# A one-column float32 matmul in front of nine of a transformer block's weight products

## The chip, the cores and the metric

The kernel runs on one core of a Trainium2 chip. The metric is the device time of one execution in microseconds. Where it is given for several runs, the median stands first and the lowest and highest behind it.

## The reference

One encoder block on 256 tokens of 2048 features, everything in float32. Cut to what matters:

```python
h = rms_norm(x, attn_norm)
proj = h @ w_in                       # 2048 x 10240: queries, keys, values, two gates
qa, ka, va, qb, kb, vb, ga, gb = jnp.split(proj, split_points, axis=-1)
ya = windowed_gqa(qa, ka, va, rel_bias_table, sink_a)        # 8 heads on 2 keys/values
yb = dilated_attention(qb, kb, vb, rel_bias_table)           # 3 groups of 4 heads
merged = sigmoid(ga) * (ya @ w_branch_a) + sigmoid(gb) * (yb @ w_branch_b)
x = x + merged @ w_out
hf = rms_norm(x, ffn_norm)
g = dwconv_centred(hf @ w_ffn_gate, conv_w, conv_b)          # 2048 x 5632
x = x + (gelu(g) * (hf @ w_ffn_up)) @ w_ffn_down
gate_p = sigmoid(rms_norm(x, ple_norm) @ w_ple_gate)
x = x + gate_p * (p @ w_ple_proj)
return rms_norm(x, final_norm)
```

## The kernel before

All weights are streamed once, in blocks of 128 by 128. A piece of 16 blocks arrives by DMA in two tiles named raw (lines 231 to 247). Each block is split into a high part whi (a ScalarE copy into the reduced float32 type, line 261) and the rest wlo (a VectorE subtraction, line 262), and the activations are kept in the same two parts. A product of two float32 matrices is then made of three products of parts: high by high, high by low, low by high.

The work is a list of jobs, _JOBS, made by _plan() and walked in order by the loop at line 1003. A job is one product with its weights. Two kinds of job matter here:

- The ordinary product (lines 330 to 335) has one block column of weights: a query or key head, or 128 features of the MLP's gate ("g") or up ("u") projection. It takes a PSUM accumulator acc of 512 columns out of three and calls block() 16 times, once for each 128 of the 2048 inputs. block() (lines 318 to 328) issues two matmuls with the weights as the stationary operand: line 324, whi against 512 columns (both parts of the 256 tokens), and line 325, wlo against the 256 columns of the high part.
- The wide product (lines 349 to 385) has the activations as the stationary operand and up to 512 columns of weights as the moving one: the values ("v"), the attention gates, the branches and the last stage. Lines 359 to 361 are its three matmuls. The products with w_out and w_ffn_down are made in a similar way by seven_product (lines 387 to 441; lines 410 to 412).

The order of the jobs is: seven queries and keys together (the first stage), values, the remaining queries of the first attention, keys, queries and values of the second attention in turn, the gates and branches, w_out ("o"), the MLP's first half (three gate products together, "gg", and then gate and up products in turn), w_ffn_down's first half ("d0"), the MLP's second half, which starts at job _HALF, w_ffn_down's second half ("d1"), and the per-layer embedding. A job's aftermath (soft-max, transposes at line 685 and at line 878, norms) is put into later jobs: at((i, k), f) asks that f be called before block k of job i, and run_due calls it. So short groups of other matmuls stand in the middle of a product: the sums of squares at line 472 (float32, one column each), the spreading of a norm at line 500 (float32, 256 columns), the scores and values of the attention at lines 631 to 644 and 700.

Each engine has one queue. The order within a queue is made by a planner that walks the instructions by priority and by planned times. keep (line 223) pins an instruction behind the one issued before it on the same engine. Semaphores are placed by the framework. ones is a 128 by 128 float32 tile of ones in SBUF (line 205).

Of the kernel before, what the change touches and what calls it, by code (L numbers as in the profile page):

```python
# [125 lines left out]
def _pairs(kind, c):  # L126

    if kind == "o":
        return ([2, 4, 5, 6, 7, 0, 1, 3] if c else [0, 1, 2, 4, 5, 6, 7, 3]), range(LATER, LATER + 4)
    if kind == "d1" and c == 1:  # L130
        return [5, 0, 1, 6, 2, 3, 7, 4, 8, 9, 10], range(5)
    return [8, 0, 1, 2, 3, 9, 4, 5, 6, 7, 10], range(SAVED)


FIRST = 7
START = FIRST + 1
_JOBS = _plan()
WARM = 9
_HALF = next(i for i, j in enumerate(_JOBS) if j[0] == "g" and j[1] == FHALF)


def _stream():
# [47 lines left out]
def _encoder(ctx: ExitStack, tc, xt, pt, cols, table, onehot, mask, ident_in, last_gain, wts, xrows, out):  # L190
    nc = tc.nc
# [13 lines left out]
    ones = const.tile([P, P], F32, name="ones")  # L205
# [17 lines left out]
    keep = tc.keep_in_program_order  # L223
# [94 lines left out]
    def block(acc, m, first, last, ahead=3):  # L318

        b = state["at"]  # L320
        s, o = _SUB_OF[b]
        split_to(s + ahead)
        hi, lo = subs[s]
        nc.tensor.matmul(acc, hi[:, o, :], m, start=first, stop=False, skip_group_check=True)  # L324
        nc.tensor.matmul(acc[:, T:], lo[:, o, :], m[:, :T], start=False, stop=last, skip_group_check=True)  # L325
        state["at"] = b + 1
        if o == _SUBS[s][1] - 1:
            del subs[s]

    def product(i, moving, n):  # L330
        acc = ps.tile([P, 2 * T], F32, name="acc", bufs=3)
        for k in range(n):
            run_due(i, k)
            block(acc, moving(k), k == 0, k == n - 1)
        return acc

    def products_by_halves(i, moving):

        accs = []
        for b in range(TOGETHER * KC):  # L340
            (h, e), k = divmod(b // SUB, TOGETHER), b % SUB
            run_due(i, b)
            if h + k == 0:
                tag = "sp" if e < 2 else "acc"
                accs.append(ps.tile([P, 2 * T], F32, name="acc", tag=tag, bufs=2 if e < 2 else 3))
            block(accs[e], moving(SUB * h + k), h + k == 0, h == 1 and k == SUB - 1)
        return accs

    def wide_product(i, still, n, w, tag, places=HALVES, late=0):

        accs = [ps.tile([P, W4], F32, name="acc", tag=tag, bufs=3 if tag == "acc" else 2) for _ in places]

        def step(k, t, hi, lo):
            xh, xl = (still(k)[:, c:c + T][:, places[t]] for c in (0, T))
            acc = accs[t][:, :w * P]
            nc.tensor.matmul(acc, xh, hi, start=(k == 0), stop=False)  # L359
            nc.tensor.matmul(acc, xh, lo, start=False, stop=False)  # L360
            nc.tensor.matmul(acc, xl, hi, start=False, stop=(k == n - 1 - t * late))  # L361

        later = []
        for k in range(n):
            run_due(i, k)
            b = state["at"]
            s, o = _SUB_OF[b]
            split_to(s + 3)
            hi, lo = (m[:, o:o + w, :] for m in subs[s])
            step(k, 0, hi, lo)  # L370
            if k < n - late:
                step(k, 1, hi, lo)
            else:
                later.append((k, 1, hi, lo))
            state["at"] = b + w
            if o == _SUBS[s][1] - w:
                del subs[s]
        def rest(side=None):
            acc, c = (accs[1][:, :T], 0) if side is None else (side, T // P)
            for e, (k, t, hi, lo) in enumerate(later):  # L380
                xh, xl = (still(k)[:, c:c + T][:, places[t]] for c in (0, T))
                for i, (xs, ws) in enumerate(((xh, hi), (xh, lo), (xl, hi))):
                    nc.tensor.matmul(acc, xs, ws[:, c:c + T // P, :], start=(side is not None and e + i == 0),
                                     stop=(e + i == len(later) + 1), skip_group_check=True)
        return accs, rest
# [137 lines left out]
    def run_due(*i):  # L523
        for f, a in due.pop(i, []):
            f(*a)
# [48 lines left out]
    for step in order:  # L574
# [6 lines left out]
        while state["at"] < min(FIRST * ready, _SUBS[state["sub"]][0]):  # L581
            k, e = divmod(state["at"], FIRST)
# [256 lines left out]
    def spread_sums(n, bank, end):  # L839

        u = row()
        nc.scalar.activation(u, bank["p1"], AF.Copy)  # L842
        to_residual(n, 0, 0, u)
        last = u
        for name in ("p6", "p7"):
            v = row()
            nc.vector.tensor_tensor(v, bank[name], last, op=ALU.add)
            last, u = v, last
        u, v = u, last
        to_residual(n, 1, 0, v)  # L850
        w = row()
        nc.vector.tensor_tensor(u, bank["p5"], u, op=ALU.add)
        nc.vector.tensor_tensor(w, bank["p5"], v, op=ALU.add)
        for t, a in enumerate((u, w)):
            if end:
                q = quarter(n, t, 1)
                nc.vector.tensor_tensor(q, q, a, op=ALU.add)
            else:
                to_residual(n, t, 1, a)
# [143 lines left out]
    for i, job in enumerate(_JOBS):  # L1003
# [82 lines left out]
        if kind == "v":  # L1086
            far = n[0] >= KVH + HG
            acc, _ = wide_product(i, stills["v"], blocks, len(n), "acc", TWINS if far else HALVES)
        elif kind in ("o", "d0", "d1"):
            names = ("p2", "p3", "p4", "c22"), ("p1", "p5", "p6", "p7")  # L1090
            places = ("sp", "sp", "pt", "pt"), ("acc", "acc", "acc", "misc")
            tags = {a: b for e in range(2) for a, b in zip(names[e], places[e ^ n])}
            still, sums_at = (stills["o"], early) if kind == "o" else (lambda k: held["act"][:, k, :], shl)
            end = kind != "d0" and n == 1
            acc = seven_product(i, *_pairs(kind, n), still, lambda m, e: [a[:, e, :] for a in sums_at(m)], tags,
                                lambda bank: spread_sums(n, bank, end))
        elif kind in stills:
            tag = {"pg": ("pt", "acc"), "pp": ("sp", "acc"), "gb": ("sp", "sp"), "ga": ("acc", "acc"), "ba": ("acc", "acc"),
                   "bb": ("sp", "sp" if n == 1 else "acc")}[kind][n % 2]
            acc, rest = wide_product(i, stills[kind], blocks, 4, tag, late=8 if last else 0)  # L1100
        elif kind == "gg":
            acc = products_by_halves(i, movers["g"])
        else:
            acc = product(i, movers[kind], blocks)
# [91 lines left out]
```

## Time and profile before

| | |
|---|---|
| three runs | 1468.14 us (1465.29 to 1469.72) |
| the profiled execution | 1465.36 us |
| its span, first to last instruction | 1463.6 us |
| mean granted TensorE clock | 0.998 |
| TensorE busy | 1450.6 us (99%), 7531 matmul passes |
| VectorE, ScalarE, GpSimd busy | 1112.7, 816.2, 107.0 us |
| moved by DMA | 362.17 MB, mean 247 GB/s |

In the rows of the profile, PE is TensorE's matmul, PEld its weight load, DVE VectorE, ACT ScalarE, POOL GpSimd and SP the engine that issues most DMAs. A row names a line of the kernel, the operation, the tile written and the tiles read. A matmul's recorded duration reaches beyond the start of the next one, because matmuls are pipelined; the pace is read from the starts. One call of a float32 matmul can leave several records.

| stage | from, us | to, us |
|---|---|---|
| attention products, behind the first stage | 59 | 325 |
| gates and branches, w_out | 325 | 638 |
| MLP, first half | 638 | 885 |
| w_ffn_down, first half | 885 | 995 |
| MLP, second half | 995 | 1240 |
| w_ffn_down, second half, and per-layer embedding | 1240 | 1463 |

### The profile page before, as it was taken

The page shows a single profiled execution, that of the slowest core. Times are in us where ns is not written, and L with a number is a line of the kernel's source. Part 1 is how long each engine was busy: PE and PEld are TensorE (multiplying, and loading weights), DVE is VectorE, ACT ScalarE, POOL GpSimd, SP SyncE. Part 2 cuts the span into 40 slices and gives each one's busy share as a digit, 9 for nine tenths or more (in the row PEclk, how much of TensorE's full clock was granted, in tenths as well). Part 3 has the DMA queues.
Part 4 walks back from the last instruction along what each step waited for, and adds up shares of the span by engine and source line. Part 5 has one row for each costly group of instructions (what it writes and reads, how often), then busy time and mean ns, then how long its engine had stood idle before and what let it go on. Part 6 is the DMA issues. An engine that isn't in the chain of part 4 may idle for free.

```text
span 1463.6 us, 20762 instructions
## 1 busy us (share of the span) xinstructions
PE 1450.6 (99%) x7531; PEld 1238.4 (85%) x7531; DVE 1112.7 (76%) x1575; ACT 816.2 (56%) x1155; POOL 107.0 (7%) x178
## 2 busy tenths in 40 slices
PE   9999999999999999999999999999999999999997
PEld 8988888888888888788888887888888888788886
DVE  7686665665665668879888878897888876988665
ACT  7465444444444456666555555675555555666653
POOL 0000000001111100201011100102110100010000
PEclk9999999999999999999999999999999999999999
DMA  9654445557888977977788886989888874797652
GB/s 326 235 180 160 168 169 171 190 180 258 294 305 295 353 234 254 291 244 272 263 281 276 292 283 201 290 289 309 278 278 279 292 241 162 257 306 243 218 192 88
DMA packets 111730, 362.17 MB, mean 247 GB/s; under 512 B 12804, under 2 KB 17924, under 8 KB 111500
## 3 DMA queue, kind: packets, MB, share of 16 engines
q1 hardware_dynamic: 88908, 292.80, 58.2%
q0 software_dynamic: 20560, 63.71, 14.3%
q10 hardware_dynamic: 2160, 4.33, 0.9%
q8 instruction: 59, 0.97, 0.3%
q14 instruction: 43, 0.35, 0.1%
HBM read 324.06 MB, written 27.30 MB: 240 GB/s over the span
## 4 chain that ended last, share of the span: by engine, by line
PE 93%; DVE 1%; ACT 0%; issue 0%; POOLq 0%; POOL 0%; DVEq 0%
PE acc L324 28%; PE acc L325 14%; PE acc L360 9%; PE acc L359 9%; PE acc L361 9%; PE acc L411 7%; PE acc L410 7%; PE acc L412 7%; PE pt L685 1%; PE pt L878 0%; DVE wlo L262 0%; PE misc L700 0%; PE sp L644 0%; PE pt L900 0%; PE misc L631 0%
## 5 line engine op out<-in xcount | busy, mean ns | idle before, releaser
L262 DVE TENSOR_TENSOR wlo<-raw,whi 128x1024 fp32r<-128x1024 f32 (+2 forms) x556 | 650.9, 1182 | 289.2 <-ACT whi L261 284.2
L261 ACT ACTIVATE whi<-raw 128x1024 fp32r<-128x1024 f32 (+2 forms) x556 | 564.3, 1025 | 530.9 <-PE acc L324 191.0
L324 PE MATMUL acc<-mov,whi 128*128 128x512 f32 x1840 | 642.5, 394 | 0.0
L325 PE MATMUL acc<-mov,wlo 128*128 128x256 f32 x1840 | 514.2, 279 | 0.0
L324 PEld LDWEIGHTS acc<-mov,whi 128*128 128x128 f32 x1840 | 345.3, 188 | 76.9
L325 PEld LDWEIGHTS acc<-mov,wlo 128*128 128x128 f32 x1840 | 347.1, 189 | 0.3
L359 PE MATMUL acc<-whi,mov 128*128 128x512 f32 (+1 forms) x504 | 193.6, 384 | 0.0
L361 PE MATMUL acc<-whi,mov 128*128 128x512 f32 (+1 forms) x504 | 193.4, 384 | 0.0
L360 PE MATMUL acc<-wlo,mov 128*128 128x512 f32 (+1 forms) x504 | 193.3, 384 | 0.0
L359 PEld LDWEIGHTS acc<-whi,mov 128*128 128x128 f32 x504 | 95.2, 189 | 18.6 <-DVE first L452 0.5
L361 PEld LDWEIGHTS acc<-whi,mov 128*128 128x128 f32 x504 | 95.2, 189 | 18.5
L360 PEld LDWEIGHTS acc<-wlo,mov 128*128 128x128 f32 x504 | 95.2, 189 | 17.9
L410 PE MATMUL acc<-whi,act 128*128 128x512 f32 x207 | 80.9, 393 | 0.2 <-ACT whi L261 0.2
L411 PE MATMUL acc<-wlo,act 128*128 128x512 f32 x207 | 81.1, 392 | 0.0
L412 PE MATMUL acc<-whi,act 128*128 128x512 f32 x207 | 80.7, 390 | 0.0
L837 POOL DMA_DIRECT2D x<-row x36 | 31.0, 878 | 375.9 <-ACT row L842 255.3
L262 DVE TENSOR_TENSOR wlo<-sums,whi 128x1024 fp32r<-128x1024 f32 x37 | 45.2, 1220 | 8.5 <-ACT whi L261 8.4
L452 DVE TENSOR_TENSOR u<-acc,t 128x256 f32<-128x256 f32 x100 | 41.8, 418 | 8.4 <-ACT t L448 8.4
L410 PEld LDWEIGHTS acc<-whi,act 128*128 128x128 f32 x207 | 38.8, 188 | 9.4 <-ACT whi L261 1.5
L411 PEld LDWEIGHTS acc<-wlo,act 128*128 128x128 f32 x207 | 38.9, 188 | 9.2 <-DVE wlo L262 1.3
L411 PE MATMUL acc<-wlo,shl 128*128 128x512 f32 x116 | 45.7, 394 | 0.0
L412 PEld LDWEIGHTS acc<-whi,act 128*128 128x128 f32 x207 | 38.9, 188 | 7.9
(218 smaller groups left out, 1642.1 us busy)
## 6 DMA issues: line engine op xcount, KB each, us to landing
raw<-in_wts SPq DMA_DIRECT2D x477, 512.0 KB, 5.1
sums<-kept SPq DMA_DIRECT2D x37, 512.0 KB, 5.4
sums<-in_wts POOLq DMA_DIRECT2D x23, 512.0 KB, 7.9
kept<-sums POOLq DMA_DIRECT2D x23, 512.0 KB, 5.7
raw<-in_wts SPq DMA_DIRECT2D x39, 256.0 KB, 5.1
row<-in_wts POOLq DMA_DIRECT2D x37, 256.0 KB, 8.3
x<-row POOLq DMA_DIRECT2D x36, 256.0 KB, 7.6
two<-in_wts POOLq DMA_DIRECT2D x14, 512.0 KB, 8.2
```

What stands on the lines that cost most here:

```text
L261: nc.scalar.activation(hi, src, AF.Copy)
L262: ins = nc.vector.tensor_tensor(lo, src, hi.bitcast(F32), op=ALU.subtract)
L324: nc.tensor.matmul(acc, hi[:, o, :], m, start=first, stop=False, skip_group_check=True)
L325: nc.tensor.matmul(acc[:, T:], lo[:, o, :], m[:, :T], start=False, stop=last, skip_group_check=True)
L359: nc.tensor.matmul(acc, xh, hi, start=(k == 0), stop=False)
L360: nc.tensor.matmul(acc, xh, lo, start=False, stop=False)
L361: nc.tensor.matmul(acc, xl, hi, start=False, stop=(k == n - 1 - t * late))
L410: nc.tensor.matmul(acc, xh, hi, start=(e == 1), stop=False)
L411: nc.tensor.matmul(acc, xh, lo, start=False, stop=False)
L412: nc.tensor.matmul(acc, xl, hi, start=False, stop=(e == uses[name]))
L452: nc.vector.tensor_tensor(u, acc[:, :T], t, op=ALU.add)
L837: keep(nc.gpsimd.dma_start(quarter(n, t, c), a, accum_op=ALU.add))
```

## The change

A list SINGLE of job numbers is made beside _HALF, and product() issues one more matmul ahead of its first block where its job is in the list.

```diff
+SINGLE = [i for i, j in enumerate(_JOBS) if i > FIRST and j[0] in ("k", "q") and _JOBS[i - 1][0] == "v"]
+SINGLE += [_HALF, _HALF + 8, _HALF + 24]
+SINGLE += [next(i for i, j in enumerate(_JOBS) if j[0] == "u") + e for e in (4, 20)]
...
     def product(i, moving, n):
         acc = ps.tile([P, 2 * T], F32, name="acc", bufs=3)
+        if i in SINGLE:
+            keep(nc.tensor.matmul(acc[:, :1], ones, ones[:, :1], start=True, stop=True))
         for k in range(n):
             run_due(i, k)
             block(acc, moving(k), k == 0, k == n - 1)
```

The matmul multiplies the tile of ones with its first column and writes column 0 of the product's own accumulator. The first block writes the whole accumulator with start=True, so the sum is overwritten at once and nothing reads it. Evaluated on the job list, SINGLE holds nine numbers: 8, 15, 19 and 29 (a query or key behind a value job), 100, 108 and 124 (one gate and two up products of the second half), 61 and 77 (two gate products of the first half). In the profile before, the first blocks of these nine products start at 59.0, 125.9, 171.7, 251.3, 995.2, 1040.1, 1128.9, 679.9 and 768.7 us.

## The prediction

> **What bounds the kernel now.** I read the profile page first, then the table of who waited for whom on TensorE, and then the instructions of line 324 in many short windows. From the page:
>
> ```profile
> span 1463.6 us, 20762 instructions
> ...
> PE 1450.6 (99%) x7531; PEld 1238.4 (85%) x7531; DVE 1112.7 (76%) x1575; ACT 816.2 (56%) x1155; POOL 107.0 (7%) x178
> ...
> PEclk9999999999999999999999999999999999999999
> ...
> PE 93%; DVE 1%; ACT 0%; issue 0%; POOLq 0%; POOL 0%; DVEq 0%
> ```
>
> TensorE is busy for 99% of the span, 93% of the chain that ended last is TensorE, and its granted clock stays at the top in every slice. The waits of TensorE itself are the next thing to look at (columns: microseconds in total, times, the longest):
>
> ```profile
> PE pt L878 <- issue: 1.3, 1, 1.3
> PE misc L213 <- DVE mhalf L208: 1.1, 1, 1.1
> ...
> PE acc L410 <- ACT whi L261: 0.2, 1, 0.2
> ```
>
> There is hardly a gap in which an added matmul could hide. No wait of this table lies in front of a gate, an up or a projection product behind the first stage. So each nanosecond put into TensorE's queue at the nine places is a nanosecond of the kernel, and each nanosecond by which its steady pace changes is one too.
>
> **What the change adds.** The list SINGLE holds, by the code's job list, nine products: the four that follow an attention value job (jobs 8, 15, 19 and 29), two of the first half of the gated MLP (jobs 61 and 77) and three of its second half (jobs 100, 108 and 124). In front of each stands one float32 matmul, the ones tile against one column of it, into column 0 of the accumulator. The product's first block starts a new group there and overwrites it. Nothing is removed or moved: no DMA, no VectorE or ScalarE work. The new matmul is the first writer of the accumulator, so it takes over the wait for that buffer; the table above shows none outstanding, and behind it in TensorE's queue stands only the same product. That moved wait I cost at nothing; if its cover went (the reader of the buffer late), the product would have waited as long without the change.
>
> **Its direct price.** The kernel already has this very form once: line 472, four calls in the middle of product 8, each total[:, tokens] against one column of ones. In the timeline of TensorE (start, length in us):
>
> ```profile
> 60.65 0.28 PE L325 MATMUL acc<-mov,wlo 128*128 128x256 f32 x1
> 60.77 0.40 PE L324 MATMUL acc<-mov,whi 128*128 128x512 f32 x1
> 61.01 0.28 PE L325 MATMUL acc<-mov,wlo 128*128 128x256 f32 x1
> 61.13 0.97 PE L472 MATMUL misc<-ones,tot 128*128 128x1 f32 x8
> 61.96 0.48 PE L324 MATMUL acc<-mov,whi 128*128 128x512 f32 x1
> 62.27 0.28 PE L325 MATMUL acc<-mov,wlo 128*128 128x256 f32 x1
> ```
>
> Four calls left eight records, so a float32 call is two passes, each with its own weight load. A block (one line 324 and one line 325) ordinarily takes 61.01 - 60.65 = 0.36 us here; with the four calls in between, the same step takes 62.27 - 61.01 = 1.26. The four cost 0.90, one costs 0.225 us. Nine cost 2.0 us. The nearest row above is the float32 call of 256 columns at line 500:
>
> ```profile
> 1003.87 0.28 PE L325 MATMUL acc<-mov,wlo 128*128 128x256 f32 x1
> 1003.99 0.59 PE L500 MATMUL misc<-rdg,ones 128*128 128x256 f32 x2
> 1004.23 0.59 PE L324 MATMUL acc<-mov,whi 128*128 128x512 f32 x1
> 1004.66 0.28 PE L325 MATMUL acc<-mov,wlo 128*128 128x256 f32 x1
> ```
>
> It takes 0.79 where a block takes 0.35, so 0.44 for one call, 4.0 us for nine. That is the upper end; the lower is the 0.225, because a pass cannot be hidden in a queue without gaps. I take 0.225: same type, same width, same neighbours.
>
> The Trainium skill, "FP8 and Floating Point Precision", section "TensorE Precision Notes", says that a true float32 product takes four passes through the array; by that the nine would cost 4.0 us at the length of a pass here. The eight records for four calls say two, and the measurement decides. The Trainium skill, "TensorE: Matmul & The Clock Gate", section "Back-to-back issue gap", puts a matmul of 1 to 64 columns at about 60 array cycles or 25 ns; nine calls of two passes would then cost an estimated 0.45 us. The row above has eight passes in 0.90 us, 0.11 each, and I stay with it.
>
> **The pace behind the added matmul.** The larger term is not the matmul but what the blocks behind it do. Line 324 in single windows (ns shortest/median/longest; first and last start; number) shows two paces:
>
> ```profile
> L324 PE MATMUL acc<-mov,whi x257: 391/394/396, 679.6 to 768.3; 128*128 128x512 f32 x129
> L324 PE MATMUL acc<-mov,whi x337: 391/394/396, 768.3 to 884.8; 128*128 128x512 f32 x169
> L324 PE MATMUL acc<-mov,whi x257: 390/391/392, 1039.8 to 1128.5; 128*128 128x512 f32 x129
> L324 PE MATMUL acc<-mov,whi x321: 390/391/392, 1128.5 to 1239.5; 128*128 128x512 f32 x161
> L324 PE MATMUL acc<-mov,whi x85: 389/398/404, 181.2 to 210.9; 128*128 128x512 f32 x85
> L324 PE MATMUL acc<-mov,whi x57: 393/398/404, 251.3 to 271.0; 128*128 128x512 f32 x57
> L324 PE MATMUL acc<-mov,whi x24: 389/398/404, 995.2 to 1003.3; 128*128 128x512 f32 x24
> ```
>
> In the first row 256 steps take 88.7 us, 0.3465 us a block; the next three give the same within their rounding. In the fifth row 84 steps take 29.7 us, 0.3536 us a block, and the last two agree. I call them the short and the long pace. Their mark in the rows is the median of line 324: 391 to 395 ns against 398 or more. The difference is 7.1 ns a block. Each pace holds for as long as nothing cuts into the blocks. The first four rows are just the four stretches that the change opens with an added matmul and that run on undisturbed to the next one or to the end of their half: 256 + 336 + 256 + 320 = 1168 blocks, all on the short pace now. If all went over to the long one it would cost 1168 x 7.1 ns = 8.3 us (1.8, 2.4, 1.8 and 2.3).
>
> Which pace follows a cut? These are the blocks right behind a short run of passes bound by weight loads, the one-column calls of line 472 (first row) and the 128-column transposes of lines 685 and 878 (the others):
>
> ```profile
> L324 PE MATMUL acc<-mov,whi x6: 395/401/477, 62.0 to 63.8; 128*128 128x512 f32 x6
> L324 PE MATMUL acc<-mov,whi x7: 392/395/474, 77.6 to 79.7; 128*128 128x512 f32 x7
> L324 PE MATMUL acc<-mov,whi x8: 393/398/481, 176.7 to 179.2; 128*128 128x512 f32 x8
> L324 PE MATMUL acc<-mov,whi x8: 395/401/477, 220.2 to 222.7; 128*128 128x512 f32 x8
> L324 PE MATMUL acc<-mov,whi x7: 395/398/477, 280.5 to 282.7; 128*128 128x512 f32 x7
> L324 PE MATMUL acc<-mov,whi x4: 391/392/475, 641.8 to 642.9; 128*128 128x512 f32 x4
> L324 PE MATMUL acc<-mov,whi x6: 391/392/475, 643.6 to 645.5; 128*128 128x512 f32 x6
> L324 PE MATMUL acc<-mov,whi x8: 394/398/478, 647.3 to 649.9; 128*128 128x512 f32 x8
> ```
>
> The first block behind each is stretched (474 to 481 ns), and then five of eight are on the long pace and three on the short. Before the fourth of them the blocks had been on the short pace:
>
> ```profile
> L324 PE MATMUL acc<-mov,whi x19: 390/391/392, 212.8 to 219.1; 128*128 128x512 f32 x19
> L324 PE MATMUL acc<-mov,whi x61: 392/395/396, 658.8 to 679.6; 128*128 128x512 f32 x61
> ```
>
> So a cut can throw the blocks off the short pace. The second row speaks the other way: it begins behind the line 500 call at 658, as the third row of the stretches does behind that at 1004, and the short pace holds. But those calls stream 256 columns a pass, and the added one is not like them: it is one column wide, as at line 472, where the long pace followed. I therefore take about half of the four stretches over to the long pace, 4.1 us, between bounds of 0 and 8.3.
>
> There is a gain too. The products at 251.3 and 995.2 start on the long pace, and the added matmul may end it: 57 x 7.1 ns = 0.4 us up to the next cut, and 24 x 7.1 = 0.17. Two more of the nine start on it:
>
> ```profile
> L324 PE MATMUL acc<-mov,whi x6: 395/398/403, 59.0 to 60.8; 128*128 128x512 f32 x6
> L324 PE MATMUL acc<-mov,whi x12: 389/399/403, 171.7 to 175.5; 128*128 128x512 f32 x12
> ```
>
> These are cut again after 6 and 12 blocks, 0.1 us each at most. In all at most 0.8; I take 0.5.
>
> **The sum.** 2.0 + 4.1 - 0.5 = +5.6 us. The profiled execution took 1465.36 us, its span 1463.6 and 1.8 around it, so it would take 1471.0. The runs shown have a median of 1468.14 (1465.29 to 1469.72), 2.8 above the profiled one, and no view says why. Carried to the median the sum is 1473.7 us, +0.38%. About 0.3%, 4.4 us, is what a measurement of this kernel can tell from no change.
>
> **The rivals.**
> Direct cost alone: the short pace survives the cut, as it did at 643.6, and the price is 2.0 - 0.5 = 1.5 us, giving 1469.6. For it speak the three short recoveries; against it the five long ones, and line 472 itself. Not slower; it decides if at most one of the four stretches changes.
> The added matmul sets the short pace, as line 500 seems to. In the profiled execution that yields the 0.8 at most against 2.0. But the runs spread by 4.4 us, and the first half's two stretches alone, 592 blocks, would make 4.2 us on the long pace; so the unprofiled runs may contain long stretches that a later cut would end. If the median's 2.8 are of that kind, the result is 1468.14 + 2.0 - 0.8 - 2.8 = 1466.5, and up to 1.6 lower if the highest run is the usual one (1464.9). Against it: in this profile there is no such stretch.
> All four stretches go over to the long pace: 2.0 + 8.3 - 0.5, 1477.9.
> The planner, which orders each engine's queue by planned times, could place other work differently because of nine more instructions, or drop the effect of the order asked for. The diff pins each new matmul behind the TensorE instruction before it, so I give this little.
>
> **How the numbers follow.** The forecast, two or more of the four stretches on the long pace, has 0.52, the case of all four included; direct cost alone 0.30; the reset 0.14; another order 0.04. Slower by over 0.3% takes the forecast and a little of the rest: 0.55. Within 0.3% takes nearly all of the direct cost and part of the reset: 0.33. Faster by over 0.3% takes what is left of the reset and of another order: 0.12. The range goes from the reset at the median (1466.5, rounded down to 1466) to all four stretches long with a microsecond of the direct cost's upper bound (1479).
>
> **What would show it.** In the profile after, each added call shows as two records of one column in front of line 324, and 0.22 to 0.23 us between the neighbouring blocks beyond one block. The four stretches show their pace in the median of line 324: 398 for long, 391 to 395 for short, and in (last start - first start) over the steps. The forecast is wrong if all four stay at 391 to 395, or if the direct price per call is far from 0.225, or if the time moves in a stage that holds no added matmul.

## The result and the profile after

| | kernel before | changed kernel |
|---|---|---|
| median | 1468.31 us (1463.68 to 1470.0, 10 runs) | 1472.65 us (1471.38 to 1474.86, 10 runs) |
| ratio | | 1.0038, 95% interval 1.0027 to 1.005 |
| profiled execution, span | 1465.36, 1463.6 us | 1474.86, 1473.1 us |

The change makes the kernel slower by 4.3 us, 0.38%; 1473.7 us had been forecast, between 1466 and 1479. Three lines move down ahead of the engine code and two more inside product(): lines 324 and 325 are 327 and 328 now, and the added call is line 336. From the page after:

```profile
span 1473.1 us, 20796 instructions
...
PE 1460.7 (99%) x7549; PEld 1241.5 (84%) x7549; DVE 1115.1 (76%) x1575; ACT 815.2 (55%) x1155; POOL 107.0 (7%) x178
...
PE 94%; DVE 1%; ACT 0%; issue 0%; POOLq 0%; POOL 0%; DVEq 0%; ACTq 0%
```

TensorE has 18 passes more than before and 10 us more of busy time. The counts of the other engines are the same, and so, instruction by instruction, is the order of the work on each engine but for the nine calls. Between the two profiles the MLP's first half grew from 246.5 to 250.9 us and its second half from 244.6 to 249.0, 8.8 of the 9.5 us by which the spans differ; what follows the second half took 0.8 us more, without an added call in it. The added line has two records a call (ns shortest/median/longest; first and last start):

```profile
L336 PEld LDWEIGHTS acc<-ones x18: 187/188/192, 58.8 to 1135.2; 128*128 128x128 f32 x18
L336 PE MATMUL acc<-ones x18: 164/208/250, 59.0 to 1135.3; 128*128 128x1 f32 x18
```

Its direct price is in the timeline of TensorE, here at job 61:

```profile
679.76 0.28 PE L328 MATMUL acc<-mov,wlo 128*128 128x256 f32 x1
679.88 0.28 PE L336 MATMUL acc<-ones 128*128 128x1 f32 x2
680.02 0.48 PE L327 MATMUL acc<-mov,whi 128*128 128x512 f32 x1
680.33 0.28 PE L328 MATMUL acc<-mov,wlo 128*128 128x256 f32 x1
```

From one line 328 to the next it takes 0.57 us where a block takes 0.35: 0.22, nine times 2.0 us. The pace of the blocks behind it is the other part. These are the four stretches of the MLP in the changed kernel, and two shorter ones, at the entries behind a wide product (an entry is the first run of blocks behind it):

```profile
L327 PE MATMUL acc<-mov,whi x256: 395/398/477, 680.0 to 770.2; 128*128 128x512 f32 x128
L327 PE MATMUL acc<-mov,whi x335: 395/398/476, 770.7 to 888.8; 128*128 128x512 f32 x168
L327 PE MATMUL acc<-mov,whi x257: 392/398/478, 1044.2 to 1134.9; 128*128 128x512 f32 x129
L327 PE MATMUL acc<-mov,whi x320: 395/398/481, 1135.4 to 1248.2; 128*128 128x512 f32 x160
L327 PE MATMUL acc<-mov,whi x25: 392/395/475, 999.7 to 1008.1; 128*128 128x512 f32 x25
L327 PE MATMUL acc<-mov,whi x57: 395/398/478, 251.6 to 271.4; 128*128 128x512 f32 x57
```

All four have a median of 398 where they had 391 and 394. In the first, 255 steps take 90.2 us, 0.3537 a block against 0.3465, with the stretched first block among them. Without that block the starts give 0.3533 in all four against 0.3467 before: 6.7 ns a block. The third row also holds the block in front of the call. The entry at _HALF (999.7) went over to the short pace, that at 251.6 stayed long.

### The profile page after: what moved, and what is told of

The parts are those of the page before. It is cut to its first block, busy times and chain, and to the rows that moved or that the text cites. A ratio compares the mean times of both kernels' runs of the same rounds, so it can differ in the third digit from the quotient of the medians.

```text
span 1473.1 us, 20796 instructions
## 1 busy us (share of the span) xinstructions
PE 1460.7 (99%) x7549; PEld 1241.5 (84%) x7549; DVE 1115.1 (76%) x1575; ACT 815.2 (55%) x1155; POOL 107.0 (7%) x178
## 4 chain that ended last, share of the span: by engine, by line
PE 94%; DVE 1%; ACT 0%; issue 0%; POOLq 0%; POOL 0%; DVEq 0%; ACTq 0%
PE acc L327 29%; PE acc L328 14%; PE acc L366 9%; PE acc L364 9%; PE acc L365 9%; PE acc L416 7%; PE acc L415 7%; PE acc L417 7%; PE pt L690 0%; PE pt L883 0%; DVE wlo L265 0%; PE sp L649 0%; PE misc L705 0%; PE pt L905 0%; PE misc L636 0%
## 5 line engine op out<-in xcount | busy, mean ns | idle before, releaser
L327 PE MATMUL acc<-mov,whi 128*128 128x512 f32 x1840 | 650.8, 398 | 0.0
```

## The experiments

In all of them a block's pace is read as above: short has a median of 391 to 395 for the line of the first matmul in block(), long has 398 or 399. A call or a group of passes that stands between two blocks is named an interruption; it throws the pace when short blocks in front of it are followed by long ones. The times of the kernel before beside each group of runs had medians of 1468.0 to 1468.6.

**The kernel before, once more**, no edit.

> The kernel before, unchanged, beside itself, profiled once more. It asks whether the long pace already occurs in the gate and up products of the kernel before in executions that the first profile does not show: its ten runs lie in two groups, 1463.7 to 1465.4 and 1468.0 to 1470.0, some 4.3 us apart, which is one half of the MLP on the long pace (592 or 576 blocks at 7 ns). Theory of the two paces: a profile with a time of 1468 or more has one half's blocks at 0.3533 us with a line 324 median of 398; a profile near 1464 to 1465 has none. Rival, the groups come from transfers or stalls elsewhere: a profile at 1468 or more has both halves at 0.3467, and the time lies in other rows.

1467.81 us (1463.3 to 1470.38, 12 runs), ratio 0.9996 (0.9982 to 1.001). The profiled execution took 1468.01 us, 2.65 more than the first profile, and has this:

```profile
L324 PE MATMUL acc<-mov,whi x654: 395/398/582, 656.5 to 887.4; 128*128 128x512 f32 x164
L324 PE MATMUL acc<-mov,whi x679: 391/391/586, 1006.9 to 1242.2; 128*128 128x512 f32 x170
```

The first half's 654 blocks run on the long pace, from the call of line 500 to the end, 230.9 / 653 = 0.3536 us each; the second half is short. From start to start the long pace is a cycle of three blocks, two of 0.35 us and one of 0.36 (the timelines of the last experiment show it). So the kernel before has the long pace in some executions of itself. Over all 99 executions of it beside these runs and the changed kernel 31 lie below 1466 (median 1464.48), 63 above 1467.3 (median 1468.72) and 5 between: two groups 4.2 us apart, where 654 blocks at 6.7 ns make 4.4. The first profile was of the smaller group.

**Only the four calls of the long stretches.**

```diff
+SINGLE = [_HALF + 8, _HALF + 24]
+SINGLE += [next(i for i, j in enumerate(_JOBS) if j[0] == "u") + e for e in (4, 20)]
```

> Only the four added matmuls in front of the long stretches (jobs 61, 77, 108, 124). Theory, the pace behind the cut is the main cost: all four stretches long, 4 x 0.22 + 8.1 = about 9 us over a run of the kernel before that has no long stretch, so 1473 to 1474 and about as slow as the whole change, within 1.5 us. Rival, the direct price and the wait handling of nine calls make the loss: four calls cost 0.9 us and the time lies within 1 us of the kernel before.

1471.93 us (1470.93 to 1473.16), ratio 1.0032 (1.002 to 1.0045). All four stretches are long; the first and the third:

```profile
L326 PE MATMUL acc<-mov,whi x256: 395/398/477, 678.3 to 768.5; 128*128 128x512 f32 x128
L326 PE MATMUL acc<-mov,whi x256: 395/398/478, 1042.9 to 1133.1; 128*128 128x512 f32 x128
```

Four calls with 0.9 us of direct price give 3.9 of the 4.3 us of the whole change, so the rival by direct price falls. The time is 1.1 us below the lower end of what was expected.

**Only the other five calls** (jobs 8, 15, 19, 29 and 100).

> Only the other five added matmuls (jobs 8, 15, 19, 29, 100). Theory, the pace behind the cut is the main cost: 5 x 0.22 = 1.1 us less up to 0.8 of entries that go over to the short pace, so +0.3 to +1.1 us on the kernel before. Rival, the direct price of nine calls makes the loss evenly: five ninths of 4.3, +2.4 us.

1468.74 us (1462.97 to 1470.35, 12 runs), ratio 1.0004 (0.9991 to 1.0017). That is 0.7 us more on the medians, which this measurement cannot tell from zero; its interval ends at 2.5 us, so the rival's 2.4 is not excluded by this run alone, only by the run with four calls. In its profile the halves are left as in the repeated profile of before:

```profile
L326 PE MATMUL acc<-mov,whi x654: 395/398/582, 656.0 to 887.0; 128*128 128x512 f32 x164
L326 PE MATMUL acc<-mov,whi x679: 392/395/579, 1006.5 to 1241.8; 128*128 128x512 f32 x170
```

**The four calls 256 columns wide**, in float32, from a second tile of ones (against the run with four calls).

```diff
+    broad = const.tile([P, T], F32, name="broad")
+    nc.vector.memset(broad, 1.0)
...
-            keep(nc.tensor.matmul(acc[:, :1], ones, ones[:, :1], start=True, stop=True))
+            keep(nc.tensor.matmul(acc[:, :T], ones, broad, start=True, stop=True))
```

> The same four places as in the run with four, but the float32 call is 256 columns wide, like that of line 500. Theory, what decides is a short pass bound by its weight load, which stretches the next block: a pass of 256 columns covers the next load, all four stretches stay at 0.3467 us a block, and the cost is four times 0.43, 1.7 us, on a kernel whose halves are both short, or less where the kernel before has a long half. Rival, any cut re-rolls the pace: some of the four stretches long, and a time like that of the run with four plus 0.8 us.

1466.86 us (1464.6 to 1467.99, 12 runs), ratio 0.9994 (0.9984 to 1.0004). The first row is in front of the first call, the others behind the first three:

```profile
L328 PE MATMUL acc<-mov,whi x62: 395/398/582, 658.6 to 680.3; 128*128 128x512 f32 x62
L328 PE MATMUL acc<-mov,whi x256: 392/395/577, 680.9 to 769.5; 128*128 128x512 f32 x128
L328 PE MATMUL acc<-mov,whi x335: 391/391/580, 770.1 to 886.1; 128*128 128x512 f32 x168
L328 PE MATMUL acc<-mov,whi x256: 392/395/579, 1041.7 to 1130.3; 128*128 128x512 f32 x128
```

Four wider, dearer calls at the same places leave all four stretches short, and the first one ended a long pace. Against the one-column version this is 5 us less.

**128 columns instead of one**, float32, the four places.

```diff
+            keep(nc.tensor.matmul(acc[:, :P], ones, ones, start=True, stop=True))
```

> The four places again, the float32 call 128 columns wide instead of one. Theory, a short pass bound by its weight load throws the pace: 128 columns still take less than the next weight load (the transposes of 128 columns stand 0.11 us apart like the one-column passes), so all four stretches long, 0.3533 us a block, as with one column. Rival, the single column and its odd offset do it: 128 columns leave the short pace, 0.3467.

One execution, 1471.19 us; a single time says little here, and the reading goes by the stretches, as in the next two runs. Three of them are long and, against the expectation, one is short, although the pace in front of it was short. The first two:

```profile
L326 PE MATMUL acc<-mov,whi x257: 391/391/475, 678.2 to 767.2; 128*128 128x512 f32 x129
L326 PE MATMUL acc<-mov,whi x336: 394/398/478, 767.7 to 886.2; 128*128 128x512 f32 x168
```

So the single column is not needed; but a call of 128 columns does not always throw the pace either.

**One pass in the reduced type, 128 columns**, the four places.

```diff
+            keep(nc.tensor.matmul(acc[:, :P], moving(0)[:, :P], moving(0)[:, :P], start=True, stop=True))
```

> The four places, one pass in the reduced float32 type (the product's own first moving tile by its own first 128 columns), 128 columns wide, overwritten at once. Theory, load-bound short pass: the long pace behind all four, at a direct price of one pass, 0.11 us. Rival, it is the float32 type with its two passes: the short pace stays at 0.3467 where it was short before.

One execution, 1469.04 us, again not all four: the stretches in front of which the pace was long became short, those in front of which it was short became long. The first row is in front of the first call, the others are the first two stretches:

```profile
L326 PE MATMUL acc<-mov,whi x62: 395/398/583, 657.1 to 678.9; 128*128 128x512 f32 x62
L326 PE MATMUL acc<-mov,whi x256: 391/394/449, 679.3 to 767.7; 128*128 128x512 f32 x128
L326 PE MATMUL acc<-mov,whi x336: 394/398/444, 768.1 to 886.5; 128*128 128x512 f32 x168
```

The float32 type and its two passes are not needed to throw the pace.

**One pass in the reduced type, 256 columns**, the four places.

```diff
+            keep(nc.tensor.matmul(acc[:, :T], moving(0)[:, :P], moving(0)[:, :T], start=True, stop=True))
```

> The four places, one pass in the reduced float32 type, 256 columns wide. Theory, load-bound short pass: a pass of 256 columns covers the next load, so the short pace stays at 0.3467 behind those of the four that start on it; price 0.12 us each. Rival, only the float32 call of 256 columns sets the short pace: some of the four long.

One execution, 1465.13 us: all four short, the first from a long pace before it.

```profile
L326 PE MATMUL acc<-mov,whi x256: 392/394/400, 679.2 to 767.6; 128*128 128x512 f32 x128
L326 PE MATMUL acc<-mov,whi x336: 391/391/396, 768.1 to 884.2; 128*128 128x512 f32 x168
```

The longest of line 326 is 400 and 396 here, not 475 to 477: nothing behind such a pass is stretched.

**The changed kernel with such a pass right behind each of its nine calls.**

```diff
             keep(nc.tensor.matmul(acc[:, :1], ones, ones[:, :1], start=True, stop=True))
+            keep(nc.tensor.matmul(acc[:, :T], moving(0)[:, :P], moving(0)[:, :T], start=True, stop=True))
```

> The changed kernel with all its nine one-column calls, and behind each of them one pass in the reduced float32 type, 256 columns wide, overwritten too. Theory, the calls cost 0.22 us each and the rest of the loss is the long pace behind them: the wide pass ends it, all four stretches short at 0.3467, and the time is that of a kernel before without a long half, 1464.3, plus nine times 0.22 + 0.12, so about 1467, some 5.5 us below the changed kernel though it issues more. Rival, the calls themselves are dear in a way that the trace does not show: the changed kernel's 1472.5 plus 1.1.

1473.24 us (1472.7 to 1474.58), ratio 1.004 (1.0025 to 1.0056): a miss. The wide pass itself was now the stretched one, 0.20 us to the next start instead of 0.12, and three stretches are long:

```profile
769.10 0.37 PE L337 MATMUL acc<-mov 128*128 128x256 f32 x1
769.30 0.40 PE L327 MATMUL acc<-mov,whi 128*128 128x512 f32 x1
```

The first two stretches of the same kernel, one short and one long; in front of the short one the pace had been long:

```profile
L327 PE MATMUL acc<-mov,whi x256: 390/391/396, 680.2 to 768.6; 128*128 128x512 f32 x128
L327 PE MATMUL acc<-mov,whi x336: 394/399/404, 769.3 to 887.7; 128*128 128x512 f32 x168
```

The time agrees with the count of long blocks all the same: 1464.5 + 9 x 0.34 + 912 x 6.7 ns = 1473.7.

**The changed kernel with such a pass in front of the two products that follow** each of jobs 61, 77, 108 and 124.

```diff
+        elif i - 1 in SINGLE[-4:] or i - 2 in SINGLE[-4:]:
+            keep(nc.tensor.matmul(acc[:, :T], moving(0)[:, :P], moving(0)[:, :T], start=True, stop=True))
```

> The changed kernel with all nine one-column calls; in front of each of the two products that follow jobs 61, 77, 108 and 124, one pass in the reduced float32 type, 256 columns wide, overwritten at once (eight passes, 0.12 us each). In the run that put such a pass directly behind the one-column call the pass itself was the stretched one (0.20 us) and three stretches stayed long; standing between two ordinary blocks such a pass left the short pace 6 of 6 times. Theory: each of the four stretches runs long for 16 to 32 blocks and then short, so the time is that of a kernel before with a short first half, 1464.3, plus 9 x 0.22, plus 8 x 0.12, plus 4 x 16 to 32 blocks at 7 ns, 1467.7 to 1468.2, some 4.5 us below the changed kernel although it issues eight matmuls more. Rival, the loss lies in the nine calls and not in the blocks behind them: 1472.6 + 1.0.

1470.61 us (1469.81 to 1472.73, 12 runs), ratio 1.0022 (1.0012 to 1.0033): 2 us below the changed kernel with eight matmuls more, and 2.5 above what was expected. Two of the four stretches are short, two long:

```profile
L327 PE MATMUL acc<-mov,whi x16: 392/395/475, 678.8 to 684.1; 128*128 128x512 f32 x16
L327 PE MATMUL acc<-mov,whi x16: 395/398/478, 768.0 to 773.4; 128*128 128x512 f32 x16
L327 PE MATMUL acc<-mov,whi x304: 387/398/403, 779.7 to 886.7; 128*128 128x512 f32 x152
```

The short ones were never thrown (first row): there the one-column call met a long pace and ended it. Where it met a short pace and threw it (second row), both wide passes behind it failed (third row). Each came two blocks behind the block of 0.36 us, and the second, 16 blocks after the first, met that same place again.

**Two wide float32 calls in the first half, no one-column call** (jobs 58 and 59).

```diff
+SINGLE = [next(i for i, j in enumerate(_JOBS) if j[0] == "u") + e for e in (1, 2)]
...
+            keep(nc.tensor.matmul(acc[:, :T], ones, broad, start=True, stop=True))
```

> No one-column call; instead one float32 call of 256 columns in front of each of the first two products behind the norm of the MLP's first half (jobs 58 and 59). The long pace repeats every three blocks, and in the profiles so far the 256-column call behind a long stretch left the long pace at only one of the three places in that cycle; from the short pace it left the short one 6 of 6 times. The two calls are 16 blocks apart, which is another place of the cycle, so both cannot miss. Theory: the first half's 654 blocks run at 0.3467 behind the second call in every execution, the times lie in one group near 1464.3 + 0.9 = 1465.2, and the median is 2 to 3 us below the kernel before. Rival, the groups of the kernel before do not come from the first half alone: two groups as before, shifted by +0.9 us.

1465.21 us (1464.33 to 1467.3, 12 runs), ratio 0.9987 (0.9974 to 0.9999). Ten of twelve lie between 1464.3 and 1465.8. The two others, 1466.61 and 1467.3, are in neither group, and what they are stays open. The pace in front of the first call and behind the second:

```profile
L327 PE MATMUL acc<-mov,whi x14: 395/398/583, 657.2 to 662.0; 128*128 128x512 f32 x14
L327 PE MATMUL acc<-mov,whi x624: 391/391/580, 668.6 to 884.7; 128*128 128x512 f32 x156
```

**The same with one pass in the reduced type.**

> As the run with two 256-column calls behind the norm of the first half (jobs 58 and 59), but one pass in the reduced float32 type each, 0.12 us instead of 0.43. Theory: the first half on the short pace in every execution, one group of times near 1464.6, median some 3.5 us below the kernel before. Rival, the cheaper pass sets the pace only from some places of the long cycle, and two groups remain.

1464.46 us (1462.75 to 1465.28, 12 runs), ratio 0.9982 (0.997 to 0.9993): one group.

**Line 500 one block later, nothing added.**

```diff
-            rms([(i, 36), (i + 1, 2), (_HALF + 1, 9)], lambda: rowsums(held["ss1"]), 1, 2)
+            rms([(i, 36), (i + 1, 3), (_HALF + 1, 9)], lambda: rowsums(held["ss1"]), 1, 2)
```

> The kernel before with nothing added: the float32 call of 256 columns that spreads the norm (line 500) is asked for before block 3 instead of block 2 of the first up product. Theory, what follows such a call is set by its place in the long pace's cycle of three blocks: at block 2 six of ten profiles so far met the one place that keeps the long pace, two another, and two the short pace; one block later the six meet a place that ends it, so that the first half is short in nearly all executions: one group near 1464.3, 3 to 4 us below the kernel before. Rival, the result is not tied to the place: two groups as before, median 1468.

1464.31 us (1463.2 to 1465.48, 12 runs), ratio 0.9976 (0.9966 to 0.9986). All twelve lie in the lower group. It beats both kernels and issues nothing more than the one before. The place of the call is seen in the timelines, first in the repeated profile of before:

```profile
655.16 0.40 PE L324 MATMUL acc<-mov,whi 128*128 128x512 f32 x1
...
655.52 0.40 PE L324 MATMUL acc<-mov,whi 128*128 128x512 f32 x1
...
655.87 0.40 PE L324 MATMUL acc<-mov,whi 128*128 128x512 f32 x1
...
656.22 0.59 PE L500 MATMUL misc<-rdg,ones 128*128 128x256 f32 x2
```

then with the call one block later:

```profile
656.88 0.40 PE L324 MATMUL acc<-mov,whi 128*128 128x512 f32 x1
...
657.23 0.40 PE L324 MATMUL acc<-mov,whi 128*128 128x512 f32 x1
...
657.59 0.59 PE L500 MATMUL misc<-rdg,ones 128*128 128x256 f32 x2
```

The long pace is a cycle of two blocks of 0.35 us and one of 0.36. In the first timeline the call stands two blocks behind the one of 0.36, and 654 long blocks follow. In the second timeline it stands right behind the one of 0.36, and this follows:

```profile
L324 PE MATMUL acc<-mov,whi x653: 392/395/577, 657.8 to 884.1; 128*128 128x512 f32 x164
```

## Why the prediction was right or wrong

The direct price held: 0.22 us a call, two passes each, 2.0 us for nine. That it could not be hidden held too.

The mechanism held: a one-column call throws the blocks behind it onto the long pace, and the four undisturbed stretches carry most of the loss. The run with four calls shows that, and the run with five agrees.

The size of the pace term was wrong: 4.1 us for half of the four stretches, where the profile after has all four long, 1168 blocks at 6.7 ns, 7.8 us. The step that failed is the tally of recoveries, which put one-column calls and transposes, from whatever pace, into one count. What they start from decides. In the profiles, a one-column call directly between two blocks led from the short pace to the long one six times of six, and from the long pace it led back to the short one only right behind the 0.36 us block.

Line 472, the prediction's nearest example, had thrown nothing: the blocks in front of it, at 59.0 in the kernel before, are long already. In the changed kernel the same four calls (line 477 there) meet a short pace and leave it short, as in the three other profiles in which they meet one. The blocks in front of them and behind them:

```profile
L327 PE MATMUL acc<-mov,whi x6: 391/391/477, 59.1 to 60.9; 128*128 128x512 f32 x6
L327 PE MATMUL acc<-mov,whi x6: 391/391/483, 62.1 to 63.9; 128*128 128x512 f32 x6
```

So what was forecast for the single added call came true, but the row it was taken from does not show it; that is luck too.

"Carried to the median" failed as well, the other way. The 2.8 us between the profiled execution and the median, of which no view of the one profile said why, are most likely a first half that runs long in about two thirds of the executions of the kernel before: the times fall into two groups, and the two last runs, which make the first half short, leave only the lower one. The rival of the reset named this possibility; its other half, that a one-column call sets the short pace, did not come true in the four stretches. Of the 7.8 us the kernel before pays 4.2 already, on its upper group. So the two errors cancel, and that the forecast came within 1.1 us of the median is partly luck. From the lower group, 1464.5 + 2.0 + 7.8 less 0.5 for the entries is 1473.8; the forecast came to 1473.7 by half the stretches on top of a higher start.

The changed kernel's median is 1 us below that sum and 2 us below its own profile. A part of this is scatter: behind the second half this profile took 224.6 us where the other thirteen took 223.7 to 224.1, and its MLP began at 638.6, late among the fourteen (636.4 to 638.9). The rest stays open; no unprofiled execution shows its stretches.

The gain at entries was taken at 0.5 us. The profile after has 85 blocks behind the transposes at 181.7 now short and 60 at 285.3 now long, beside the two entries named, so what a call changes there reaches beyond the next cut, where the prediction let it end. The run with five calls gives +0.7 us on medians with an interval that spans zero, against 1.1 of direct price. That agrees with 0.5 and does not prove it.

## What to carry to other kernels

On an engine without gaps the pace of a long undisturbed stretch is worth more than any single instruction: 6.7 ns on 1168 blocks against 0.22 us a call. Look for it in the start-to-start times, not in busy time, and take several profiles of an unchanged kernel before a difference of 0.3% is put down to an edit. In this kernel an extra pass of 1 or 128 columns could throw the pace for hundreds of blocks. One of 256 columns between two blocks did not throw it, but did not always end a long pace either. Moving an interruption by one block was worth 4 us, as much as the best added calls gave.

## What the runs showed of the hardware

Blocks of one matmul of 512 and one of 256 columns ran at two fixed paces, 0.3467 and 0.3533 us, at the same granted clock of 0.998 to 0.999; the short one was kept for up to 679 blocks and the long one for 654. The long one is a cycle of three blocks. The Trainium skill, "TensorE: Matmul & The Clock Gate", section "Back-to-back issue gap", gives for an isolated warm matmul a gap of its columns at 2.4 GHz plus 2.5 ns, an estimated 0.325 us for the two of such a block. No stretch here ran at that.

What follows a float32 call of 256 columns was repeatable by its place. The short pace outlasted it in every profile where the call met it. On the long pace it ended the long cycle right behind the block of 0.36 us and one block later, and kept it two blocks later (nine profiles). The reduced pass of 256 columns agreed at the two places where it stood: it ended the long cycle right behind that block (twice) and kept it two blocks later (four times). Entries from a wide product at 0.2267 us a matmul, with a one-column call between, began short, and those from one at 0.2333 began long (six and three entries, in three profiles); without the call both begin long.

A float32 call, two records, cost 0.21 to 0.23 us at 1 and at 128 columns and 0.42 to 0.44 at 256; one pass in the reduced type cost 0.11 to 0.13 at 128 and 0.12 to 0.14 at 256. The prediction took the two records of a call for its two passes. At 256 columns the call costs more than three reduced passes of that width, so the records do not settle how often the columns are streamed. Why the cycle exists was not tried; no run here looks below the starts of the instructions.
